# Zero-padded second score products, the mixer's input re-laid through DRAM, and a reorder with one spare tile

## Chip, cores and metric

One core of a Trainium2 chip runs the kernel. TensorE multiplies, VectorE and ScalarE evacuate and do elementwise work, GpSimd helps with small pieces, and nearly all transfers are issued from SyncE's queue (SP). The metric is device time in microseconds (us) of one execution; the median of several runs counts.

## The reference, cut to what matters

Two transformer blocks on a sequence of 1024 tokens of width 1024, in float32. The first has a gated spatial mixer, three groups of dilated window attention and attention to 256 memory tokens. The second has three branches, which the change touches:

```
h = rms_norm(x) * (1 + scale) + shift                     # (1024, 1024)
u, z_ssm, qd, kd, vd, z_diff, qs, ks, vs, z_swa = split(h @ w_in)
# mixer: u is (1024, 16 groups, 16); per group a complex diagonal state of 64
st[t] = a * st[t-1] + B u[t];  y = Re(C st) + d * u;  y = gelu(y) * sigmoid(...)
# differential attention: 4 heads, each two score maps of head dim 64, causal
p = softmax(q1 k1 + bias) - lam * softmax(q2 k2 + bias);  o = rms_norm(p @ v)
# sliding-window attention: 4 query heads on 2 key heads of dim 64, window 128, sinks
x = x + gate * (concat(y_ssm, y_diff, y_swa) @ w_out)
```

## The kernel before

**Precision.** TensorE gets 32-bit values in its fast float32 form, split in two: a high part (hi) and the rest (lo). A dense product is three products, hi x hi, hi x lo and lo x hi, summed in PSUM. ScalarE makes hi by a copy, VectorE lo by a subtraction (`hilo`, and `w_conv` for weights). The normed input lies transposed, channels on partitions, as `hTh` and `hTl` (in the second block `h2Th` and `h2Tl`): 8 tiles of 128 channels x 1024 tokens.

**Units.** `unitA` holds 128 tokens of h as the weights in the array and streams 256 weight columns: 8 x 3 products of 256 columns into PSUM with tokens on partitions. `unitB` holds 128 weight columns and streams 512 tokens: 8 x 3 products of 512 columns, with channels on partitions. A continuation evacuates the PSUM tile.

**The order.** A planner in the kernel (`Sched`) runs coroutines against modelled costs when the program is built, so that the order on each engine is fixed then; the engines execute it in order. Counted resources stand for buffers: `t4` (tiles of 128 x 1024; 20 at first, 24 after `fewer_w` has run twice in the second block), `mm` and `x` (four PSUM tiles each), `raw` (three weight buffers), `whl` (converted weights). `acq` takes them and `rel` gives them back. The dense products are one coroutine, `dense`; a block of attention is one each. The profile gives one line to all instructions of a helper: L239 is a matmul, L249 a transpose, L156 every instruction of VectorE, ScalarE and GpSimd, L253 every transfer. So the tile names tell the place.

**The reorder.** In the first block h is stored with its tokens reordered by a stride of 4 (the second dilation). Group 0 needs plain order. `reorder` does that in place for each of the 8 channel tiles, hi and lo: ScalarE copies hi with a stride into `cvh`, and VectorE copies it back plainly; VectorE copies lo with a stride into `cvl`, and ScalarE copies it back plainly. It holds two spare tiles. TensorE's group 0 products wait for it, and so do the memory products queued beside it.

**The mixer's u.** `dense_u` runs eight `unitA` with the weights being every eighth token of h: unit j takes the tokens 8c + j. ScalarE puts the results into `U` with tokens c on partitions, reversed in j. `ssm` transposes 16 pieces of `U` into `UT`, so that partitions hold 8 steps x 16 channels of a group; from there come input products (`wi`), a scan on VectorE (`scan`, `St`), output products with the tables `T` and `WoZ`, an activation (`Yg`), transposes (`Yn`), and a hi/lo split (`ygh`, `ygl`) that the gated unit (`dense_glu`) reads. The tables are made from powers of a in `ssm_prep`, a stage in the background.

**The second score products.** A query is split into hi and lo, a key too. For differential attention `K[sx]` holds the key's hi in 64 partitions and its lo in the other 64, and `dQh` the query's hi twice, so one product of 128 rows gives hi x hi + hi x lo. The second product, query lo x key hi, takes 64 rows:

```
self.mm(ps[:, :wn], self.dQh[th][:, sx, qs], H.K[sx][:, ks], True, False)
self.mm(ps[:, :wn], self.dQl[hs, th, qs], H.K[sx][hs, ks], False, True)
```

The sliding window does the same with the roles changed: `wQ` holds hi and lo, `wK` hi twice, and `wKl` the key's lo in 64 partitions.

Of the kernel before, what the change touches and what calls it, by code (L numbers as in the profile page):

```python
# [180 lines left out]
class Kern:  # L181
# [508 lines left out]

    def reorder(self, k, ev):

        yield from self.acq("t4", 2)
        for eng, src, name in ((0, self.hTh[:, k], "cvh"), (1, self.hTl[:, k], "cvl")):
            t = self.t4(F32R, name)
            o, i = t.rearrange("p (m r) -> p m r", r=4), src.rearrange("p (r m) -> p m r", r=4).bitcast(F32)
            if eng == 0:
                self.A.activation(o, i, AF.Copy)
                yield
                self.V.tensor_copy(src, t.bitcast(F32))  # L700
            else:
                self.V.tensor_copy(o, i)
                yield
                self.A.activation(src, t.bitcast(F32), AF.Copy)
            yield
        self.rel("t4", 2)
        ev.t = self.s.cur.t

    def bias_prep(self):
# [828 lines left out]
    def ssm_prep(self):  # L1538
# [119 lines left out]

        V.tensor_add(dm, self.ident[0:32, 0:16], self.ident[0:32, 16:32])
        G.memset(Bz, 0.0)  # L1660
        yield
        for pr in range(8):
            tt_ = (tc_, td)[pr % 2]
            EB = tt_[:, 0:256].rearrange("p (c k h) -> p c k h", c=2, k=8)
            CA = tt_[:, 256:544].rearrange("p (c k h) -> p c k h", c=2, k=9)
            we = tt_[:, 544:800]
            Gm = tb[0:32, 768:1024]
            tt = [t2[:, i, 0:128].rearrange("p (a b) -> p a b", a=8) for i in range(2)]
            pb = lambda c, n: pw[:, pr, c, 0:n, None].to_broadcast([P, n, 16])
            self.cmul(EB[:, 0], EB[:, 1], bb[:, 0, pr, None, :].to_broadcast(sh), bb[:, 1, pr, None, :].to_broadcast(sh),  # L1670
                      pb(0, 8), pb(1, 8), tt)
            yield
            yield from self.acq("x")
            ps = self.ps("x")
            for c in range(2):
                self.tr(ps[:, c * P:(c + 1) * P], EB[:, c].rearrange("p a b -> p (a b)"))
            yield
            A.activation(we, ps[:, 0:256], AF.Copy)
            self.rel("x")
            t = self.s.cur.t  # L1680
            self.dma(self.Win_d[:, pr].rearrange("p c q -> p (c q)"), we, 128)
            self.s.cur.t = t
            sh9 = [P, 9, 16]
# [12 lines left out]
            for c in range(2):  # L1696
                self.mm(ps[0:32, 0:P], Bz[:, c, :], CA[:, c, 0:8, :].rearrange("p a b -> p (a b)"), c == 0, c == 1)
            G.memset(Gm[:, 0:P], 0.0)
            yield
            V.tensor_copy(Gm[:, 144:256], ps[0:32, 16:P])  # L1700
            V.scalar_tensor_tensor(Gm[:, P:144], dm, dcol[:, pr:pr + 1], ps[0:32, 0:16], op0=OP.mult, op1=OP.add)
            self.rel("x")
            t = self.s.cur.t
            self.dma(self.G_d[pr], Gm, 32)
            self.s.cur.t = t
            yield
# [165 lines left out]
    def dense_u(self):  # L1872
        s = self.s
        hh, hl = self.hk()
        yield from self.acq("t4", 6)

        U = [self.t4(F32, "U").rearrange("p (g k h) -> p g k h", g=8, k=8) for _ in range(2)]
        left = [8]
        done = Ev()
        w = self.w["u"]  # L1880
        for j in range(8):
            def cont(ps, j=j):
                for i in range(2):
                    self.A.activation(U[i][:, :, 7 - j, :], ps[:, i * P:(i + 1) * P].rearrange("p (g h) -> p g h", g=8),
                                      AF.Copy)
                self.rel("mm")
                left[0] -= 1
                if left[0] == 0:
                    done.t = s.cur.t
                yield  # L1890
            yield from self.unitA(w, hh, hl, slice(j, j + 8 * 127 + 1, 8), self.h_ev if j == 0 else [], cont, 20)
        w.done()
        self.glu_ev = Ev()
        self.zs, self.zs_ev = {}, {}
        s.spawn(self.ssm(U, done), 21, "ssm")

    def ssm(self, U, done):
        I, s, V, A, G = self.I, self.s, self.V, self.A, self.G
        yield done
        yield self.ssmp_ev  # L1900
        A8t = self.cp.tile([P, 7, 3, 8], F32, name="A8")
        self.dma(A8t, self.A8_d, 84)
        gb = self.cp.tile([P, 2], F32, name="glub")
        self.dma(gb, I["glu_b_2"].rearrange("o (e p) -> p (o e)", p=P), 1)
        UT = [self.t4(F32, "UT").rearrange("p (g c) -> p g c", g=8) for _ in range(2)]
        for q in range(4):
            yield from self.acq("x")
            ps = self.ps("x")
            for g in range(4):
                self.tr(ps[:, g * P:(g + 1) * P], U[q // 2][:, q % 2 * 4 + g].rearrange("p k h -> p (k h)"))  # L1910
            yield
            A.activation(UT[q // 2][:, q % 2 * 4:q % 2 * 4 + 4, :], ps.rearrange("p (g c) -> p g c", g=4), AF.Copy)
            self.rel("x")
        self.rel("t4")
        St = [self.t4(F32, "St").rearrange("p (r c) -> p r c", r=8) for _ in range(2)]

# [27 lines left out]
        def load(q):  # L1944
            T, WoZ = Ts[q % 2], Ws[q % 2]
            for k in range(8):

                self.dma(T[16 * k:16 * k + 16],
                         bass.AP(tensor=self.G_d.tensor, offset=self.G_d.offset + q * 2 * 32 * 256 + P - 16 * (7 - k),
                                 ap=[[256, 16], [32 * 256, 2], [16 * 256, 2], [1, P]]), 32)  # L1950
            for s_ in range(2):
                for pr in (2 * q, 2 * q + 1):
                    self.dma(WoZ[pr % 2][s_ * 64:(s_ + 1) * 64, s_], self.Wo_d[s_ * 64:(s_ + 1) * 64, pr], 64)
            yield
            t_ev[q].t = s.cur.t
# [180 lines left out]
    def diff_alloc(self, H):  # L2136
# [5 lines left out]
        H.kalloc.t = self.s.cur.t  # L2142
        if h == 0:

            yield from self.acq("t4", 4)
            self.dbias = self.t4(F32, "dbias")
            self.G.iota(self.dbias, pattern=[[1, 1024]], base=-896, channel_multiplier=-1,
                        allow_small_or_imprecise_dtypes=True)
# [2 lines left out]
            yield  # L2151

            self.dQh = [self.t4(F32R, "dQh").rearrange("p (s t) -> p s t", s=2) for _ in range(2)]
            self.dQl = self.t4(F32R, "dQl").rearrange("p (h t) -> p h t", h=2)
        H.balloc.t = self.s.cur.t
        for th in range(2):
            if h:
# [3 lines left out]
    def dense_diff(self, h, heads):  # L2161
# [42 lines left out]
        def units_q(th):  # L2204
            tsl = slice(th * 512, (th + 1) * 512)

            def cont(ps):
# [3 lines left out]
                for sx in range(2):  # L2211
# [1 line left out]
                    src, q = ps[hs], self.dQh[th][:, sx]  # L2213
                    A.activation(q[hs], src, AF.Copy, scale=f)
                    yield
                    V.scalar_tensor_tensor(self.dQl[hs, th], src, f, q[hs].bitcast(F32), op0=OP.mult, op1=OP.subtract)
                    A.activation(q[64 - sx * 64:128 - sx * 64], src, AF.Copy, scale=f)
                    yield
                self.rel("mm")
# [46 lines left out]
    def diff_block(self, H, i, before):  # L2266
# [21 lines left out]
        def stream(sx):  # L2288
            sc = pr[sx]
            for ch in range(nch):  # L2290
# [2 lines left out]
                wn = max(wd, 256)  # L2293
                yield from self.acq("x")
                ps = self.ps("x")
                qs, ks, hs = slice(i % 4 * P, (i % 4 + 1) * P), slice(c0, c0 + wn), slice(sx * 64, (sx + 1) * 64)
                self.mm(ps[:, :wn], self.dQh[th][:, sx, qs], H.K[sx][:, ks], True, False)
                self.mm(ps[:, :wn], self.dQl[hs, th, qs], H.K[sx][hs, ks], False, True)
                yield
                bo = 896 - i * P + c0  # L2300
                V.tensor_tensor_reduce(out=sc[:, c0:c0 + wd], in0=ps[:, :wd], in1=self.dbias[:, bo:bo + wd], scale=1.0,
# [70 lines left out]
        if H.left == 0:  # L2372
# [1 line left out]
            self.spill_y(2 + h, H.z)  # L2374
            self.rel("t4", 3)
            if h == 3:
                self.rel("t4", 4)

    def z_alloc(self, H):
        yield from self.acq("t4")  # L2380
# [10 lines left out]

    def swa_alloc(self, W_):
        I, V, G = self.I, self.V, self.G
        yield from self.acq("t4", 3)

        W_.K, W_.Kl = [self.t4(F32R, "wK") for _ in range(2)], self.t4(F32R, "wKl")
        W_.kalloc.t = self.s.cur.t
        yield from self.acq("t4", 1)
        W_.V = self.t4(F32, "wV").rearrange("p (b v) -> p b v", b=8)
# [18 lines left out]
    def dense_swa(self, H3):  # L2418
# [8 lines left out]
        for th in range(2):  # L2427
            tsl = slice(th * 512, (th + 1) * 512)

            def cont(ps, th=th, tsl=tsl):  # L2430
                yield W_.kalloc
                for sx in range(2):
# [2 lines left out]
                    hi = W_.K[sx][hs, tsl]  # L2435
                    A.activation(hi, src, AF.Copy)
                    yield
                    V.tensor_sub(W_.Kl[hs, tsl], src, hi.bitcast(F32))
                    A.activation(W_.K[sx][64 - sx * 64:128 - sx * 64, tsl], src, AF.Copy)
                    yield  # L2440
                self.rel("mm")
# [68 lines left out]
    def swa_block(self, W_, b, before):  # L2510
# [19 lines left out]
        def pair(kv):  # L2530
            yield from self.acq("x")
            psS = self.ps("x").rearrange("p (s k) -> p s k", s=2)
            for sx in range(2):
                q, hs = W_.Q[th][kv][:, sx, b % 4 * P:(b % 4 + 1) * P], slice(kv * 64, (kv + 1) * 64)
                self.mm(psS[:, sx, :], q, W_.K[kv][:, c0:c0 + 256], True, False)
                self.mm(psS[:, sx, :], q[hs], W_.Kl[hs, c0:c0 + 256], False, True)
            yield
            for sx in range(2):
                h = 2 * kv + sx
# [37 lines left out]
        if W_.left[th] == 0:  # L2577
            self.rel("t4", 2)
            if th:
                self.rel("t4", 7)  # L2580
        yield
        while (th, 1) not in self.wz_ev:
            yield lambda: (th, 1) in self.wz_ev
# [229 lines left out]
```

## Time and profile before

| | |
|---|---|
| median of 3 runs | 1868.13 us (1867.87 to 1875.78) |
| profiled execution | 1873.96 us, span 1871.5 us |
| TensorE busy | 1826.0 us (98%) |
| VectorE, ScalarE, GpSimd busy | 54%, 38%, 7% |
| TensorE's mean granted clock | 0.977 of 2.4 GHz |
| moved by DMA | 145.80 MB |

Busy time counts from the start to the end of instructions; those of TensorE overlap, so its pace is read from start to start. The span is the time from the first to the last instruction; the execution's own time is a little longer.

### The profile page before, as it was taken

The page shows a single profiled execution, that of the slowest core. Times are in us where ns is not written, and L with a number is a line of the kernel's source. Part 1 is how long each engine was busy: PE and PEld are TensorE (multiplying, and loading weights), DVE is VectorE, ACT ScalarE, POOL GpSimd, SP SyncE. Part 2 cuts the span into 40 slices and gives each one's busy share as a digit, 9 for nine tenths or more (in the row PEclk, how much of TensorE's full clock was granted, in tenths as well). Part 3 has the DMA queues.
Part 4 walks back from the last instruction along what each step waited for, and adds up shares of the span by engine and source line. Part 5 has one row for each costly group of instructions (what it writes and reads, how often), then busy time and mean ns, then how long its engine had stood idle before and what let it go on. Part 6 is the DMA issues. An engine that isn't in the chain of part 4 may idle for free.

```text
span 1871.5 us, 28564 instructions
## 1 busy us (share of the span) xinstructions
PE 1826.0 (98%) x11071; PEld 1599.5 (85%) x11071; DVE 1007.1 (54%) x2674; ACT 713.3 (38%) x1648; POOL 136.2 (7%) x203
## 2 busy tenths in 40 slices
PE   7999599999999999999999999999999999999998
PEld 6999599998899878878888889999877687777798
DVE  5657755655666776521322334550486735554575
ACT  5454753543414222111211222661334434534543
POOL 1313202210000000000000000010000000000000
PEclk9999799999999999999999999999999998998899
DMA  6212131112232225611212212530202110101442
GB/s 217 73 64 69 35 114 46 35 37 68 71 117 61 57 65 165 197 48 46 91 45 77 76 62 91 170 117 14 68 29 57 46 57 12 46 23 68 168 139 76
DMA packets 163722, 145.80 MB, mean 78 GB/s; under 512 B 17996, under 2 KB 149630, under 8 KB 163588
## 3 DMA queue, kind: packets, MB, share of 16 engines
q1 hardware_dynamic: 163588, 143.99, 24.6%
q8 instruction: 87, 1.43, 0.3%
q14 instruction: 47, 0.39, 0.1%
HBM read 123.57 MB, written 22.75 MB: 78 GB/s over the span
## 4 chain that ended last, share of the span: by engine, by line
PE 94%; DVE 3%; ACT 2%; DMA 1%; issue 0%; SPq 0%; POOLq 0%; POOL 0%; DVEq 0%; ACTq 0%
PE psmm L239 76%; PE psx L239 13%; PE psx L249 4%; ACT cvh L156 1%; DMA xt<-in_x_dram 1%; DVE dp L156 1%; DMA t<-in_rel_bias_dram 0%; ACT wsc L156 0%; SPq L253 0%; ACT hTl L156 0%; DVE Q L156 0%; ACT dp L156 0%; DVE zs L156 0%; DVE wlo L156 0%; DVE dst L156 0%
## 5 line engine op out<-in xcount | busy, mean ns | idle before, releaser
L156 DVE TENSOR_TENSOR wlo<-wraw,whi 128x1024 fp32r<-128x1024 f32 (+3 forms) x161 | 183.2, 1138 | 224.5 <-ACT whi L156 215.7
L239 PE MATMUL psmm<-hTh,whi 128*128 128x512 f32 x672 | 266.0, 396 | 0.0
L239 PE MATMUL psmm<-whi,hTh 128*128 128x256 f32 x896 | 263.4, 294 | 1.4 <-ACT hTh L156 1.4
L239 PE MATMUL psmm<-hTl,whi 128*128 128x512 f32 x672 | 262.0, 390 | 0.0
L239 PE MATMUL psmm<-hTh,wlo 128*128 128x512 f32 x672 | 262.0, 390 | 0.0
L239 PE MATMUL psmm<-whi,hTl 128*128 128x256 f32 x896 | 254.9, 284 | 0.0
L239 PE MATMUL psmm<-wlo,hTh 128*128 128x256 f32 x896 | 254.7, 284 | 0.0
L239 PEld LDWEIGHTS psmm<-whi,hTh 128*128 128x128 f32 x896 | 173.8, 194 | 2.5 <-ACT hTh L156 1.8
L239 PEld LDWEIGHTS psmm<-wlo,hTh 128*128 128x128 f32 x896 | 174.1, 194 | 0.1
L239 PEld LDWEIGHTS psmm<-whi,hTl 128*128 128x128 f32 x896 | 173.6, 194 | 0.2 <-DVE hTl L156 0.2
L156 ACT ACTIVATE whi<-wraw 128x1024 fp32r<-128x1024 f32 (+3 forms) x161 | 158.7, 989 | 33.8 <-PE psmm L239 19.3
L239 PEld LDWEIGHTS psmm<-hTh,wlo 128*128 128x128 f32 x672 | 126.2, 188 | 26.9
L239 PEld LDWEIGHTS psmm<-hTh,whi 128*128 128x128 f32 x672 | 126.2, 188 | 26.6 <-issue 1.8
L239 PEld LDWEIGHTS psmm<-hTl,whi 128*128 128x128 f32 x672 | 126.3, 188 | 24.6
L156 ACT ACTIVATE tg<-psmm,gb 128x512 f32<-128x512 f32 x48 | 33.1, 689 | 283.2 <-PE psmm L239 258.6
L239 PE MATMUL psmm<-h2Th,whi 128*128 128x512 f32 x320 | 140.3, 439 | 0.0
L239 PE MATMUL psmm<-h2Tl,whi 128*128 128x512 f32 x320 | 129.5, 405 | 0.0
L239 PE MATMUL psmm<-h2Th,wlo 128*128 128x512 f32 x320 | 129.3, 404 | 0.0
L156 POOL TENSOR_TENSOR hst<-hst,mhalf 128x4 f32<-128x4 f32 (+1 forms) x68 | 68.5, 1011 | 257.8 <-DVE hst L156 246.1
L239 PEld LDWEIGHTS psmm<-h2Th,whi 128*128 128x128 f32 x320 | 62.7, 196 | 18.5 <-issue 7.3
L239 PEld LDWEIGHTS psmm<-h2Th,wlo 128*128 128x128 f32 x320 | 62.7, 196 | 14.4
L156 DVE CUSTOM_DVE_ANT_0 dp<-psx,dbias 128x512 f32<-128x512 f32 (+3 forms) x96 | 52.6, 555 | 40.7 <-PE psx L239 39.7
(355 smaller groups left out, 3817.7 us busy)
## 6 DMA issues: line engine op xcount, KB each, us to landing
wraw<-in_w_in_dram SPq DMA_DIRECT2D x96, 512.0 KB
wraw<-in_w_out_dram SPq DMA_DIRECT2D x32, 512.0 KB
ada<-in_ada_w_dram SPq DMA_DIRECT2D x24, 512.0 KB
wraw<-in_m_w_kv_dram SPq DMA_DIRECT2D x8, 512.0 KB
x2t<-in_x_dram SPq DMA_DIRECT2D x8, 512.0 KB
x_d<-x2t SPq DMA_DIRECT2D x8, 512.0 KB
xt<-in_x_dram SPq DMA_DIRECT2D x7, 512.0 KB
og_d<-rows SPq DMA_DIRECT2D x24, 132.0 KB
```

Of the source, the lines that this page charges most:

```text
L156: r = real(*a, **k)
L239: self.nc.tensor.matmul(out, lhsT, rhs, start=start, stop=stop)
L249: self.nc.tensor.transpose(out, in_, self.ident[:k, :k])
```

## The change

1. `reorder`: for hi and lo in turn, ScalarE copies the tile plainly into one spare tile, and VectorE copies it back with the stride.
2. `dense_u`: four `unitB` instead of eight strided `unitA`. ScalarE writes the PSUM tile with tokens regrouped (j, c) into `U`; each half of `U` is stored to DRAM (`u0_d`, `u1_d`), and `ssm` loads it back in 8 pieces of 16 partitions as `UT`. The 16 transposes go. Since the order of the 8 steps isn't reversed any more, the tables are made from reversed powers (`pwr`) and loaded in the other order.
3. The second score products take 128 rows: `dQl` and `wKl` become a pair of tiles each, in which the 64 partitions not used are set to zero once. One more `t4` is held for each pair.

```
 def reorder(self, k, ev):
+        for src in (self.hTh[:, k], self.hTl[:, k]):
+            yield from self.acq("t4")
+            t = self.t4(F32R, "cv")
+            self.A.activation(t, src.bitcast(F32), AF.Copy)
+            yield
+            self.V.tensor_copy(src.rearrange("p (m r) -> p m r", r=4),
+                               t.rearrange("p (r m) -> p m r", r=4).bitcast(F32))
+            yield
+            self.rel("t4")
...
+        pwr = tc_[:, 800:928].rearrange("p (r c k) -> p r c k", r=8, c=2)
+        for k in range(8):
+            V.tensor_copy(pwr[:, :, :, k], pw[:, :, :, 7 - k])
...
 def dense_u(self):
+        for e in range(2):
+            left = [2]
+            for th in range(2):
+                def cont(ps, e=e, th=th, left=left):
+                    self.A.activation(U[e][:, :, th * 64:(th + 1) * 64], ps.rearrange("p (c j) -> p j c", j=8), AF.Copy)
+                    self.rel("mm")
+                    left[0] -= 1
+                    if left[0] == 0:
+                        yield
+                        self.dma(self.u_d[e], U[e].rearrange("p j c -> p (j c)"))
+                        done[e].t = s.cur.t
+                    yield
+                yield from self.unitB(w, slice(e * P, (e + 1) * P), hh, hl, slice(th * 512, (th + 1) * 512),
+                                      [self.h_ev[4 * th + 3]] * 8, cont, 20)
...
 def ssm(self, done):
+        for e in range(2):
+            yield done[e]
+            for j in range(8):
+                self.dma(UT[e][16 * j:16 * j + 16], bass.AP(tensor=self.u_d[e].tensor, offset=self.u_d[e].offset + j * P,
+                                                            ap=[[S, 16], [16 * S, 8], [1, P]]), 64)
-        for q in range(4):
-            yield from self.acq("x")
-            ps = self.ps("x")
-            for g in range(4):
-                self.tr(ps[:, g * P:(g + 1) * P], U[q // 2][:, q % 2 * 4 + g].rearrange("p k h -> p (k h)"))
...
 def diff_alloc(self, H):
-            yield from self.acq("t4", 4)
+            yield from self.acq("t4", 5)
+            self.dQl = [self.t4(F32R, "dQl").rearrange("p (h t) -> p h t", h=2) for _ in range(2)]
+            for sx in range(2):
+                self.G.memset(self.dQl[sx][64 - sx * 64:128 - sx * 64].bitcast(F32), 0.0)
...
 def diff_block(self, H, i, before):
-                self.mm(ps[:, :wn], self.dQl[hs, th, qs], H.K[sx][hs, ks], False, True)
+                self.mm(ps[:, :wn], self.dQl[sx][:, th, qs], H.K[sx][:, ks], False, True)
...
 def swa_alloc(self, W_):
-        yield from self.acq("t4", 3)
+        yield from self.acq("t4", 4)
+        W_.K, W_.Kl = [[self.t4(F32R, n) for _ in range(2)] for n in ("wK", "wKl")]
+        for sx in range(2):
+            G.memset(W_.Kl[sx][64 - sx * 64:128 - sx * 64].bitcast(F32), 0.0)
...
 def swa_block(self, W_, b, before):
-                self.mm(psS[:, sx, :], q[hs], W_.Kl[hs, c0:c0 + 256], False, True)
+                self.mm(psS[:, sx, :], q, W_.Kl[kv][:, c0:c0 + 256], False, True)
```

## Rows read from the trace of the kernel before

**Rows 1.** The page: busy us, share of the span and instructions of each engine.

```profile
PE 1826.0 (98%) x11071; PEld 1599.5 (85%) x11071; DVE 1007.1 (54%) x2674; ACT 713.3 (38%) x1648; POOL 136.2 (7%) x203
```

**Rows 2.** Busy time by stretch: length, engines, granted clock, DMA share, GB/s.

```profile
200.00:240.00 40.00, 20.12 (x97) 16.21 (x96) 31.34 (x97) 34.08 (x68) 5.84 (x10) 0.62 0.12 37
...
1340.00:1400.00 60.00, 60.00 (x271) 44.97 (x270) 53.96 (x186) 19.89 (x47) 2.97 (x5) 1.00 0.09 27
...
1500.00:1700.00 200.00, 198.93 (x991) 154.28 (x990) 98.37 (x299) 84.05 (x200) 11.80 (x21) 0.96 0.11 35
1700.00:1776.00 76.00, 75.92 (x380) 59.21 (x381) 36.35 (x134) 36.17 (x107) 0.00 (x0) 0.82 0.35 122
```

**Rows 3.** Timeline of TensorE at 1342 us: start, duration, instruction.

```profile
1342.43 0.49 PE L239 MATMUL psx<-dK,dQl 64*128 64x512 f32 x1
1342.86 0.49 PE L239 MATMUL psx<-dK,dQh 128*128 128x512 f32 x1
...
1343.70 0.50 PE L239 MATMUL psmm<-h2Th,whi 128*128 128x512 f32 x1
1344.04 0.39 PE L239 MATMUL psmm<-h2Tl,whi 128*128 128x512 f32 x1
1344.27 0.39 PE L239 MATMUL psmm<-h2Th,wlo 128*128 128x512 f32 x1
```

**Rows 4.** The same at 1696 us, sliding-window scores, fourteen rows of the pattern left out.

```profile
1696.28 0.28 PE L239 MATMUL psx<-wK,wQ 128*128 128x256 f32 x1
1696.49 0.38 PE L239 MATMUL psx<-wKl,wQ 64*128 64x256 f32 x1
...
1701.17 0.58 PE L239 MATMUL psx<-wK,wQ 128*128 128x256 f32 x1
1701.68 0.58 PE L239 MATMUL psx<-wKl,wQ 64*128 64x256 f32 x1
```

**Rows 5.** The same at 196 us, scores of the first block.

```profile
196.84 0.64 PE L239 MATMUL psx<-K,Q 128*128 128x256 f32 x4
197.31 0.28 PE L239 MATMUL psmm<-whi,hTh 128*128 128x256 f32 x1
```

**Rows 6.** By tile, dQl and wKl: ns min/median/max, first and last start, forms.

```profile
L239 PE MATMUL psx<-dK,dQl x96: 379/492/793, 1335.6 to 1675.3; 64*128 64x512 f32 x48, 64*128 64x256 f32 x32, 64*128 64x384 f32 x16
...
L239 PE MATMUL psx<-wKl,wQ x32: 378/481/581, 1696.5 to 1752.7; 64*128 64x256 f32 x32
```

**Rows 7.** By tile, U.

```profile
L156 ACT ACTIVATE U<-psmm x16: 272/275/277, 1276.9 to 1317.5; 128x128 f32<-128x128 f32 x16
...
L249 PE MATMUL psx<-ident,U x16: 272/273/273, 1319.3 to 1320.9; 128*128 128x128 f32 x16
```

**Rows 8.** Timeline of TensorE at 1317 us, where the products of u end.

```profile
1316.91 0.41 PE L239 MATMUL psmm<-whi,h2Tl 128*128 128x256 f32 x1
1317.16 0.28 PE L239 MATMUL psmm<-whi,h2Th 128*128 128x256 f32 x1
1317.28 0.28 PE L239 MATMUL psmm<-wlo,h2Th 128*128 128x256 f32 x1
```

**Rows 9.** Busy time by stretch, while the mixer's tables are loaded.

```profile
1328.00:1344.00 16.00, 16.00 (x104) 12.18 (x103) 6.48 (x24) 4.99 (x23) 0.00 (x0) 1.00 0.34 90
```

**Rows 10.** By tile, ygl and ygh: the mixer's end and the gated unit.

```profile
L156 DVE TENSOR_TENSOR ygl<-psx,ygh x4: 672/685/691, 1447.0 to 1454.7; 128x512 fp32r<-128x512 f32 x4
...
L239 PE MATMUL psmm<-ygh,whi x8: 389/436/502, 1460.0 to 1469.1; 128*128 128x512 f32 x8
```

**Rows 11.** By tile, cvh and cvl: the reorder's copies.

```profile
L156 ACT ACTIVATE cvh<-hTh x8: 1948/1998/2097, 197.6 to 222.7; 128x1024 fp32r<-128x1024 f32 x8
L156 DVE CAST hTh<-cvh x8: 683/694/695, 205.9 to 230.3; 128x1024 fp32r<-128x1024 f32 x8
...
L156 DVE CAST cvl<-hTl x8: 1164/1204/1312, 209.0 to 235.4; 128x1024 fp32r<-128x1024 f32 x8
L156 ACT ACTIVATE hTl<-cvl x8: 1047/1058/1071, 211.4 to 236.6; 128x1024 fp32r<-128x1024 f32 x8
```

**Rows 12.** Timeline of TensorE at 228 us, with the idle time before and what ended it.

```profile
228.18 1.22 PE L239 MATMUL psx<-K,Q 128*128 128x256 f32 x4 [10.67 <-DVE Q L156]
```

More of the change, by code (lines that the diff above doesn't have):

```diff
@@ L691, in reorder @@
     def reorder(self, k, ev):
[L693 to L704, printed above, removed]
+        for src in (self.hTh[:, k], self.hTl[:, k]):
+            yield from self.acq("t4")
+            t = self.t4(F32R, "cv")
+            self.A.activation(t, src.bitcast(F32), AF.Copy)
             yield
-        self.rel("t4", 2)
+            self.V.tensor_copy(src.rearrange("p (m r) -> p m r", r=4),
+                               t.rearrange("p (r m) -> p m r", r=4).bitcast(F32))
+            yield
+            self.rel("t4")
         ev.t = self.s.cur.t
@@ L1670, in ssm_prep @@
             self.cmul(EB[:, 0], EB[:, 1], bb[:, 0, pr, None, :].to_broadcast(sh), bb[:, 1, pr, None, :].to_broadcast(sh),
-                      pb(0, 8), pb(1, 8), tt)
+                      *(pwr[:, pr, c, :, None].to_broadcast(sh) for c in range(2)), tt)
             yield
@@ L1875, in dense_u @@
         yield from self.acq("t4", 6)
-        U = [self.t4(F32, "U").rearrange("p (g k h) -> p g k h", g=8, k=8) for _ in range(2)]
-        left = [8]
-        done = Ev()
+        U = [self.t4(F32, "U").rearrange("p (j c) -> p j c", j=8) for _ in range(2)]
+        self.u_d = [self.dp.tile([P, S], F32, name=f"u{e}_d") for e in range(2)]
+        done = [Ev(), Ev()]
         w = self.w["u"]
[L1881 to L1891, printed above, removed]
+        for e in range(2):
[12 more added lines that the diff above has]
+                                      [self.h_ev[4 * th + 3]] * 8, cont, 20)
         w.done()
@@ L1894, in dense_u, with ssm @@
         self.zs, self.zs_ev = {}, {}
-        s.spawn(self.ssm(U, done), 21, "ssm")
-    def ssm(self, U, done):
+        s.spawn(self.ssm(done), 21, "ssm")
+    def ssm(self, done):
         I, s, V, A, G = self.I, self.s, self.V, self.A, self.G
-        yield done
+        UT = [self.t4(F32, "UT").rearrange("p (g c) -> p g c", g=8) for _ in range(2)]
+        for e in range(2):
[4 more added lines that the diff above has]
+            yield
         yield self.ssmp_ev
@@ L1904, in ssm @@
         self.dma(gb, I["glu_b_2"].rearrange("o (e p) -> p (o e)", p=P), 1)
-        UT = [self.t4(F32, "UT").rearrange("p (g c) -> p g c", g=8) for _ in range(2)]
-        for q in range(4):
-            yield from self.acq("x")
-            ps = self.ps("x")
-            for g in range(4):
-                self.tr(ps[:, g * P:(g + 1) * P], U[q // 2][:, q % 2 * 4 + g].rearrange("p k h -> p (k h)"))
-            yield
-            A.activation(UT[q // 2][:, q % 2 * 4:q % 2 * 4 + 4, :], ps.rearrange("p (g c) -> p g c", g=4), AF.Copy)
-            self.rel("x")
         self.rel("t4")
@@ L1948, in load @@
                 self.dma(T[16 * k:16 * k + 16],
-                         bass.AP(tensor=self.G_d.tensor, offset=self.G_d.offset + q * 2 * 32 * 256 + P - 16 * (7 - k),
+                         bass.AP(tensor=self.G_d.tensor, offset=self.G_d.offset + q * 2 * 32 * 256 + P - 16 * k,
                                  ap=[[256, 16], [32 * 256, 2], [16 * 256, 2], [1, P]]), 32)
@@ L2153, in diff_alloc @@
             self.dQh = [self.t4(F32R, "dQh").rearrange("p (s t) -> p s t", s=2) for _ in range(2)]
-            self.dQl = self.t4(F32R, "dQl").rearrange("p (h t) -> p h t", h=2)
+            self.dQl = [self.t4(F32R, "dQl").rearrange("p (h t) -> p h t", h=2) for _ in range(2)]
+            for sx in range(2):
+                self.G.memset(self.dQl[sx][64 - sx * 64:128 - sx * 64].bitcast(F32), 0.0)
         H.balloc.t = self.s.cur.t
@@ L2215, in cont @@
                     yield
-                    V.scalar_tensor_tensor(self.dQl[hs, th], src, f, q[hs].bitcast(F32), op0=OP.mult, op1=OP.subtract)
+                    V.scalar_tensor_tensor(self.dQl[sx][hs, th], src, f, q[hs].bitcast(F32), op0=OP.mult, op1=OP.subtract)
                     A.activation(q[64 - sx * 64:128 - sx * 64], src, AF.Copy, scale=f)
@@ L2295, in stream @@
                 ps = self.ps("x")
[L2296 removed]
+                qs, ks = slice(i % 4 * P, (i % 4 + 1) * P), slice(c0, c0 + wn)
                 self.mm(ps[:, :wn], self.dQh[th][:, sx, qs], H.K[sx][:, ks], True, False)
[L2298 removed]
+                self.mm(ps[:, :wn], self.dQl[sx][:, th, qs], H.K[sx][:, ks], False, True)
                 yield
@@ L2376, in diff_block @@
             if h == 3:
-                self.rel("t4", 4)
+                self.rel("t4", 5)
     def z_alloc(self, H):
@@ L2393, in swa_alloc @@
         I, V, G = self.I, self.V, self.G
-        yield from self.acq("t4", 3)
-        W_.K, W_.Kl = [self.t4(F32R, "wK") for _ in range(2)], self.t4(F32R, "wKl")
+        yield from self.acq("t4", 4)
+        W_.K, W_.Kl = [[self.t4(F32R, n) for _ in range(2)] for n in ("wK", "wKl")]
+        for sx in range(2):
+            G.memset(W_.Kl[sx][64 - sx * 64:128 - sx * 64].bitcast(F32), 0.0)
         W_.kalloc.t = self.s.cur.t
@@ L2437, in cont @@
                     yield
-                    V.tensor_sub(W_.Kl[hs, tsl], src, hi.bitcast(F32))
+                    V.tensor_sub(W_.Kl[sx][hs, tsl], src, hi.bitcast(F32))
                     A.activation(W_.K[sx][64 - sx * 64:128 - sx * 64, tsl], src, AF.Copy)
@@ L2533, in pair @@
             for sx in range(2):
-                q, hs = W_.Q[th][kv][:, sx, b % 4 * P:(b % 4 + 1) * P], slice(kv * 64, (kv + 1) * 64)
+                q = W_.Q[th][kv][:, sx, b % 4 * P:(b % 4 + 1) * P]
                 self.mm(psS[:, sx, :], q, W_.K[kv][:, c0:c0 + 256], True, False)
-                self.mm(psS[:, sx, :], q[hs], W_.Kl[hs, c0:c0 + 256], False, True)
+                self.mm(psS[:, sx, :], q, W_.Kl[kv][:, c0:c0 + 256], False, True)
             yield
@@ L2579, in swa_block @@
             if th:
-                self.rel("t4", 7)
+                self.rel("t4", 8)
         yield
```

## The prediction

> **What bounds the kernel now.** I read the page's engine shares first: TensorE is busy for 98% of the span [rows 1], so a change counts as far as it shortens TensorE's own queue or one of its few gaps. A busy engine may still be slow, so next came the busy times by stretch with the granted clock [rows 2]: between 200 and 240 us TensorE does nothing for half the time, and after 1500 us the clock is not always full. Third came TensorE's timeline in the three places that the change touches, read from start to start, because the ends of matmuls overlap. The reader is to see three spacings. A 512-wide score product beside one of 64 rows starts 0.43 us after the last, while plain 512-wide products follow each other at 0.23 us [rows 3]. Sixteen 256-wide score products of alternating 128 and 64 rows take 4.89 us from the first start to the start after the last, 0.306 us each, and at the lower clock 0.51 us [rows 4]. The attention of the first block makes the same hi and lo products with all 128 rows; four start within 0.47 us, 0.12 us each [rows 5]. So it is the alternation of row counts that costs, not the width or the change of weights.
>
> **Score products on 128 rows.** There are 96 second products in the differential attention, 48 of 512, 32 of 256 and 16 of 384 columns, and 32 of 256 in the sliding-window attention [rows 6]. Each is one of a pair with a 128-row product, and the pair pays twice. A 256-wide pair falls from 2 x 0.306 to 2 x 0.12, by 0.37 us; a 512-wide pair from 2 x 0.43 to 2 x 0.23, by 0.40 us [rows 3 to 5]. For 384 columns no plain row exists; it lies between the two, so I take 0.38. Sum: 64 x 0.37 + 48 x 0.40 + 16 x 0.38 = 23.7 + 19.2 + 6.1 = **49 us**. The plain product after a pair also starts 0.34 instead of 0.23 us later [rows 3]; I leave this out as reserve.
>
> A rule speaks against this. The Trainium skill, "TensorE: Matmul & The Clock Gate", Part 3 (packing small matmuls), says that products on different row groups can run at the same time, so that a half-height product can be nearly free; padding would give that up. By it this term would be a loss, worked out below as a rival. The rows here show 0.31 and 0.43 us for every half-height product and no overlap [rows 3, 4], because a full-height one stands on either side of it.
>
> **The clock.** It is 0.96 in the 200 us after 1500 and 0.82 in the 76 us after 1700 [rows 2]; 8.0 and 13.7 us of full-speed time are not granted, 21.7 in all. In the timeline the fall to 1.2 GHz at 1701 comes at the end of the sixteen alternating products [rows 4]; the plain work before that ran at 2.4 GHz. If the alternation goes, most of these falls should go. Bounds: nothing and 21.7 us. I take two thirds, **14 us**, since some falls may follow real waits.
>
> **What the other engines keep.** The work around the scores hangs on VectorE, which is busy 54 of 60 us between 1340 and 1400 [rows 2]. The 49 us lie over 418 us (1335 to 1753, [rows 6]), so 7 us fall into that stretch, and VectorE leaves 6. In the sliding-window part VectorE and ScalarE are half idle, but each block is a chain through both. Bounds: nothing lost, and 20 us, the 7 there and as much in either later stretch; I take **7 us lost**. The zeroed halves are memsets on GpSimd, which is busy for 7% of the span [rows 1], and stand once each.
>
> **The products of u.** Now eight units read every eighth token as weights; their evacuations run from 1276.9 to 1317.5 us [rows 7], two to a unit, so a unit is about 40.6 / 7 = 5.80 us, 0.242 us for each of 24 products, at full clock. The moment the weights are contiguous again, the same 256-wide product starts every 0.12 us [rows 8]; the stride, not the clock, halves the rate. The new form has the weights still and contiguous and streams 512 tokens: 4 units x 24 x 0.23 = 22.1 us [rows 3] against 8 x 5.80 = 46.4: **24.3 us** less. The 16 transposes go too; they run from 1319.3 to 1320.9 us [rows 7]: **1.7 us**. All of it stands on TensorE with nothing else running.
>
> **u through memory.** The mixer now waits for a 512 KB store and eight 64 KB loads for each half. The nearest rows are the mixer's own small loads: 90 GB/s in the 16 us after 1328 [rows 9]. The second half, 0.5 MB out and 0.5 MB back, is at that rate 5.8 + 5.8 = 12 us, against some 4 us now from the last u evacuation to the transposed copy; so the mixer is about 8 us later as seen from TensorE's queue. SP's queue waits meanwhile (the loads wait for the store), and the weight loads behind it are late by as much; three raw buffers, each of 11 us of products (2 x 24 x 0.23), cover that. What is late next is the gated unit that reads the mixer: its last input is written at 1454.7 + 0.7 and TensorE reaches it at 1460.0, 4.6 us to spare [rows 10]. TensorE will come to it earlier: 49 x 125 / 418 = 15 us of the pair saving lie before 1460. If VectorE's scan didn't get any faster, TensorE would stand there for 8 + 15 - 4.6 = 18 us; but VectorE also waits for scores in that stretch, and the planner knows of the transfers and can put other work in front. Bounds 0 and 18 us; I take **4 us lost**. The reversed powers are eight small VectorE copies in a background stage, covered by dense products.
>
> **The reorder.** ScalarE now makes 8 strided copies of 2.00 and 8 plain ones of 1.06 us, VectorE 8 of 1.20 and 8 of 0.69 [rows 11]. After it ScalarE makes 16 plain ones (17.0 instead of 24.5 us) and VectorE 16 strided ones (19.2 instead of 15.1). They stand where TensorE idles for 20 of 40 us, ScalarE is busy for 34.1 and VectorE for 31.3 [rows 2]; the longest gap, 10.7 us, ends with a Q piece that stood behind reorder copies on ScalarE [rows 12]. ScalarE falls to 26.6, VectorE rises to 35.4. The stretch shortens at most to what VectorE needs, 4.6 us; at worst VectorE's 4.1 us are added. Nearest to the rows is relief of the fuller engine: **4 us** less. Holding one spare tile instead of two can only free tiles earlier.
>
> **Tiles.** Two longer-held tiles (the second dQl, the second wKl) leave less room in a pool of 24 while head 1 is set up. The wait would stand in the dense queue before head 1's gate product. I count 25 tiles wanted there; head 0's blocks end close to it and return four. Taken as nothing; bound 11 us, the length of that gate product's two units.
>
> **Sum.** The profiled execution took 1873.96 us with a span of 1871.5. 49 + 14 - 7 + 26 - 4 + 4 = 82 us less gives 1792. The median of the runs shown is 5.8 us below the profiled one, so the forecast against it is 1868.1 - 82 = **1786 us**.
>
> **Rivals.**
> (1) The mixer and VectorE become the bound: TensorE is faster but stands before the gated unit and in the scan stretch. For it: 4.6 us to spare [rows 10], VectorE at 90%. Against: VectorE waits for scores there. Losses of 18 + 20 instead of 4 + 7 us, and no clock gained: 1786 + 27 + 14 = 1827 at its worst, about 1812 in the middle.
> (2) Padding doesn't do what it says: the stall stays, for instance because it comes from the change of weights. Then only u and the reorder help: 1868 - 26 = 1842. Against: [rows 5].
> (3) Half-height products were nearly free and each now costs its full time: 64 x 0.12 + 48 x 0.23 + 16 x 0.18 = 21.6 us more; with u and the reorder 1868 + 22 - 26 = 1864, no change. [rows 3, 4] speak against it, since nothing overlaps there. It is the packing rule of the Trainium skill, "TensorE: Matmul & The Clock Gate", Part 3, named above.
> (4) Slower: the re-laid u lands so late that TensorE, whose queue is in order, stands at the mixer's input products. The place is the first product that reads UT; every microsecond late there costs one. It decides from 82 us on. To be that late the sixteen 64 KB loads would have to land one after the other at over 5 us each. The mixer's small loads moved 1.4 MB in 16 us [rows 9], which speaks against it.
>
> **How the numbers follow.** Forecast 0.70 (its own range 1766 to 1804: all of the clock and no loss, or no clock gain and small losses); rival 1 0.17; rival 2 0.06; rival 3 0.03; rival 4 0.04. The range from 1764 to 1822 holds the forecast and most of rival 1. A measurement of this kernel tells about 0.5%, 9 us, from no change: faster 0.93, same 0.03, slower 0.04.
>
> **What the profile after would show.** Second products of 128 rows at 0.12 and 0.23 us from start to start; a clock near 1.00 after 1500; u as four units of 5.5 us; ScalarE's reorder copies all near 1.06 us and VectorE's near 1.20; little idle time on TensorE before the ygh products. A long idle row there, or in front of the products that read UT, would make the forecast wrong, as would scores that keep a spacing of 0.3 us.

## The result and the profile after

The changed kernel took 1785.37 us (median of 4 runs, 1783.57 to 1786.1) against 1868.0 for before: a ratio of 0.9549, with a 95% interval from 0.9521 to 0.9578. The profiled execution took 1786.1 us with a span of 1784.3, against 1871.5.

The page's engine shares and then the windows of after (length, engines, granted clock, DMA share, GB/s), which answer to [rows 1, 2]:

```profile
PE 1733.3 (97%) x10959; PEld 1552.2 (87%) x10959; DVE 1008.6 (57%) x2682; ACT 701.5 (39%) x1632; POOL 143.7 (8%) x207
```

```profile
200.00:240.00 40.00, 21.49 (x131) 18.67 (x130) 34.53 (x89) 27.05 (x72) 12.27 (x11) 0.66 0.12 37
1340.00:1400.00 60.00, 59.03 (x348) 50.74 (x347) 50.26 (x170) 27.84 (x63) 2.20 (x4) 1.00 0.20 58
1500.00:1700.00 200.00, 193.65 (x1159) 168.94 (x1158) 130.25 (x409) 110.86 (x279) 12.65 (x21) 0.98 0.24 80
1680.00:1700.00 20.00, 16.94 (x118) 16.35 (x119) 13.96 (x27) 9.62 (x21) 0.00 (x0) 0.83 0.34 110
```

TensorE has 112 instructions fewer, 96 products of u and the 16 transposes; the rest is the same work in less time: 93 us less busy, and 5.5 us more idle. The 0.98 after 1500 us is no longer a fall among the score products; it comes from the last 20 us, behind a wait, to which we come back.

TensorE's timeline of after, in the differential attention and in the sliding window, against [rows 3, 4]:

```profile
1301.34 0.28 PE L239 MATMUL psx<-dK,dQh 128*128 128x256 f32 x1
1301.46 0.28 PE L239 MATMUL psx<-dK,dQl 128*128 128x256 f32 x1
...
1508.36 0.39 PE L239 MATMUL psx<-dK,dQh 128*128 128x512 f32 x1
1508.59 0.39 PE L239 MATMUL psx<-dK,dQl 128*128 128x512 f32 x1
1508.82 0.40 PE L239 MATMUL psx<-dK,dQh 128*128 128x512 f32 x1
...
1659.27 0.28 PE L239 MATMUL psx<-wKl,wQ 128*128 128x256 f32 x1
1659.39 0.28 PE L239 MATMUL psx<-wK,wQ 128*128 128x256 f32 x1
```

From start to start it is 0.12 us for 256 columns and 0.23 for 512; 0.31 and 0.43 are gone.

By tile (ns min/median/max, first and last start), the copies of u, the mixer's end, the gated unit and the reorder, against [rows 7, 10, 11]:

```profile
L156 ACT ACTIVATE U<-psmm x4: 598/598/599, 1272.5 to 1288.9; 128x512 f32<-128x512 f32 x4
...
L156 DVE TENSOR_TENSOR ygl<-psx,ygh x4: 679/683/691, 1411.5 to 1421.6; 128x512 fp32r<-128x512 f32 x4
...
L239 PE MATMUL psmm<-ygh,whi x8: 389/389/475, 1430.7 to 1437.0; 128*128 128x512 f32 x8
...
L156 ACT ACTIVATE cv<-hTh x8: 1042/1046/1059, 196.9 to 215.0; 128x1024 fp32r<-128x1024 f32 x8
L156 DVE CAST hTh<-cv x8: 1180/1220/1253, 202.8 to 223.9; 128x1024 fp32r<-128x1024 f32 x8
```

A unit of u is now (1288.9 - 1272.5) / 3 = 5.47 us. The gated unit has not become a wait: its last input is written at 1421.6 + 0.7 and read at 1430.7, 8.4 us to spare instead of 4.6.

The new idle time stands where the forecast did not look. TensorE at the end of the sliding window, after (start, duration, instruction, idle time before it and what ended it):

```profile
1674.27 0.41 PE L249 MATMUL psx<-ident,wsc 128*128 128x128 f32 x2 [0.94 <-DVE wst L156]
...
1679.36 0.41 PE L249 MATMUL psx<-ident,wsc 128*128 128x128 f32 x2 [0.94 <-DVE wsc L156]
1682.20 0.58 PE L239 MATMUL psmm<-whi,yh 128*128 128x256 f32 x1 [2.43 <-ACT yh L156]
1682.58 0.42 PE L239 MATMUL psmm<-wlo,yh 128*128 128x256 f32 x1
1683.67 0.80 PE L239 MATMUL psmm<-whi,yh 128*128 128x256 f32 x2 [0.67 <-DVE yh L156]
```

Products of 256 columns that last 0.28 us elsewhere last 0.58 behind that wait: TensorE was granted the lower level, 1.2 GHz, for some 7 us (0.83 on the average of the 20 us from 1680).

### The profile page after: what moved, and what is told of

The parts are those of the page before. It is cut to its first block, busy times and chain, and to the rows that moved or that the text cites. A ratio compares the mean times of both kernels' runs of the same rounds, so it can differ in the third digit from the quotient of the medians.

```text
span 1784.3 us, 28346 instructions
## 1 busy us (share of the span) xinstructions
PE 1733.3 (97%) x10959; PEld 1552.2 (87%) x10959; DVE 1008.6 (57%) x2682; ACT 701.5 (39%) x1632; POOL 143.7 (8%) x207
## 4 chain that ended last, share of the span: by engine, by line
PE 90%; DVE 5%; ACT 2%; DMA 1%; issue 1%; POOL 0%; SPq 0%; POOLq 0%; DVEq 0%; ACTq 0%
PE psmm L239 76%; PE psx L239 10%; PE psx L249 4%; DVE dp L156 1%; ACT cv L156 1%; DVE hTl L156 1%; DVE scan L156 1%; DMA ada<-in_ada_w_dram 1%; DVE wlo L156 0%; DMA xt<-in_x_dram 0%; ACT whi L156 0%; DVE macc L156 0%; DVE zs L156 0%; DVE dK L156 0%; ACT dp L156 0%
## 5 line engine op out<-in xcount | busy, mean ns | idle before, releaser
L239 PE MATMUL psmm<-h2Th,wlo 128*128 128x512 f32 x352 | 138.0, 392 | 0.0
L239 PE MATMUL psmm<-h2Tl,whi 128*128 128x512 f32 x352 | 137.8, 391 | 0.0
L156 POOL TENSOR_TENSOR hst<-hst,mhalf 128x4 f32<-128x4 f32 (+1 forms) x68 | 69.4, 1024 | 259.4 <-DVE hst L156 247.9
L239 PEld LDWEIGHTS psmm<-h2Th,whi 128*128 128x128 f32 x352 | 66.5, 189 | 11.8 <-issue 0.2
L239 PEld LDWEIGHTS psmm<-h2Tl,whi 128*128 128x128 f32 x352 | 66.6, 189 | 10.6
```

Source lines behind the costliest of these rows:

```text
L156: r = real(*a, **k)
L239: self.nc.tensor.matmul(out, lhsT, rhs, start=start, stop=stop)
```

## The experiments

In the first four, the parts alone and a test of the stall's cause, before took 1872.68 us on the same chip.

**Padding alone.** Part 3 of the change:

```
-self.mm(ps[:, :wn], self.dQl[hs, th, qs], H.K[sx][hs, ks], False, True)
+self.mm(ps[:, :wn], self.dQl[sx][:, th, qs], H.K[sx][:, ks], False, True)
```

> Before, with the second score products padded to 128 rows and nothing else. Theory A, changing the row count stalls TensorE and the falls of the clock follow from these stalls: from the traces of before and after, 37.5 us of pair spacing and 3 us of late plain products at full clock, plus 24 us of half-clock time, less about 7 us of new idle time at the end: 1868 - 58 = 1810 us (1800 to 1818), granted clock near 1.00 after 1500 us. Theory B, the falls of the clock have another cause: only 41 us less, 1827 to 1834 us, and the clock stays near 0.82 in the last stretch before the output products. Theory C, the stall belongs to the change of weights: 1868 us.

1819.26 us (1818.15 to 1820.0), ratio 0.972 (0.9687 to 0.9754). Its windows:

```profile
1500.00:1700.00 200.00, 198.79 (x1150) 172.12 (x1150) 121.02 (x397) 105.64 (x268) 12.63 (x21) 1.00 0.17 53
1700.00:1764.00 64.00, 58.82 (x472) 57.46 (x471) 40.64 (x91) 29.44 (x73) 1.10 (x2) 0.95 0.48 165
```

The clock is 1.00 through the scores, so theory A, though 1 us beyond its range; against before on this chip it is 53 us less, where A had 58. TensorE stands idle for 15.9 us in the second block instead of 5.2, while A allowed for 7. Part of that stands at the mixer's transposes (four waits of 0.5 to 1.4 us), part is the 2.43 us wait on yh, the same as in after. In the two parts below that wait does not appear, so it comes with the padding.

**u alone.** Part 2 of the change:

```
-yield from self.unitA(w, hh, hl, slice(j, j + 8 * 127 + 1, 8), self.h_ev if j == 0 else [], cont, 20)
+yield from self.unitB(w, slice(e * P, (e + 1) * P), hh, hl, slice(th * 512, (th + 1) * 512), ..., cont, 20)
```

> Before, with u as four units and the way through memory alone; score products stay on 64 rows. Theory A, the transfers are covered: 46.4 - 22.1 + 1.7 = 26 us less, 1842 us (1838 to 1846). Theory B, the mixer arrives 8 us later against 4.6 us to spare at the gated unit, and TensorE stands there: 1846 to 1852 us, with an idle row of 3 us or more in front of the ygh products.

1847.96 us (1842.58 to 1852.38), ratio 0.9873 (0.9834 to 0.9912): 24 us less, with 17 to 31 in the interval. The time lies in B's range, but both ranges were set from 1868 us, and 1872.68 - 26 = 1847 is what A gives on this chip. The trace decides, with the mixer's end at 1436.8 + 0.7 and the gated unit at 1447.9, 10.4 us to spare and no idle row before it. Theory A.

```profile
L156 DVE TENSOR_TENSOR ygl<-psx,ygh x4: 679/683/686, 1426.6 to 1436.8; 128x512 fp32r<-128x512 f32 x4
...
L239 PE MATMUL psmm<-ygh,whi x8: 387/486/500, 1447.9 to 1455.6; 128*128 128x512 f32 x8
```

**The reorder alone.** Part 1 of the change:

```
-self.A.activation(o, i, AF.Copy)
-self.V.tensor_copy(src, t.bitcast(F32))
...
+self.A.activation(t, src.bitcast(F32), AF.Copy)
+self.V.tensor_copy(src.rearrange("p (m r) -> p m r", r=4), t.rearrange("p (r m) -> p m r", r=4).bitcast(F32))
```

> Before, with the reorder alone. Theory A, ScalarE's relief is worth what the landmarks of before and after show between 154 and 588 us: 4 us less, 1864 us (1862 to 1866). Theory B, it is an accident of the planner's order with the other two edits, or only the 0.8 us earlier start: 1867 to 1870 us.

1865.82 us, ratio 0.9983 (0.9962 to 1.0004): 3 us less, not clear of noise by the time. By the trace the last product of whi and hTh starts 575.5 us after the first transpose (584.8 - 9.3) instead of 579.0 (588.6 - 9.6), 3.5 us earlier. The other traces agree: 575.1 to 575.5 us in four with these copies (after and two edits of it among them), 578.0 to 579.2 us in four without. So A, by the traces.

**Fewer changes of row count.** Before, with every other pair reversed:

```
-self.mm(psS[:, sx, :], q, W_.K[kv][:, c0:c0 + 256], True, False)
-self.mm(psS[:, sx, :], q[hs], W_.Kl[hs, c0:c0 + 256], False, True)
+hi, lo = (q, W_.K[kv][:, c0:c0 + 256]), (q[hs], W_.Kl[hs, c0:c0 + 256])
+first, last = (hi, lo) if sx else (lo, hi)
+self.mm(psS[:, sx, :], *first, True, False)
+self.mm(psS[:, sx, :], *last, False, True)
```

(and the other way round in the differential attention).

> Before, with 64-row second products kept, but every other pair reversed (first, second, second, first), so that where pairs adjoin, equal row counts adjoin and the changes of row count are halved. Theory A, each change of row count costs: a 64-row product behind a 64-row one starts at most 0.12 us (256 columns) or 0.23 us (512) after it, and the time falls by up to half of 42 us and of 24 us of clock: 1833 to 1855 us. Theory B, each 64-row product costs by itself: spacing and time stay, 1868 us. Theory C, products on different halves of the rows overlap: the second 64-row product starts 0.05 us or less after the first.

1832.79 us (1832.12 to 1834.53), ratio 0.9794 (0.9761 to 0.9828), with the same 128 products of 64 rows. Its timeline (x2 is two instructions in one row):

```profile
1671.49 0.50 PE L239 MATMUL psx<-wK,wQ 128*128 128x256 f32 x2
1671.91 0.39 PE L239 MATMUL psx<-wKl,wQ 64*128 64x256 f32 x2
1672.23 0.50 PE L239 MATMUL psx<-wK,wQ 128*128 128x256 f32 x2
...
1677.55 0.38 PE L239 MATMUL psx<-wKl,wQ 64*128 64x256 f32 x1
1677.86 0.50 PE L239 MATMUL psmm<-h2Th,whi 128*128 128x512 f32 x1
```

Two things are to be seen. A cycle of four products takes 1672.23 - 1671.49 = 0.74 us instead of 4 x 0.306 = 1.22, with two changes of row count instead of four; so each change costs some 0.2 us, and theory A holds. And two 64-row products take 0.32 us to the next start where one takes 0.31: the second is nearly free, as in theory C; one by one in the trace, it starts 0.003 us after the first. The two stand on different halves of the rows and write different PSUM tiles. B, by which spacing and time stay, falls.

The changes were not halved in all: where other work came between the pairs they did not adjoin. In the trace 39 of the 128 products of 64 rows stand right behind another, and the changes fell from 256 to 178. That the time still came out just below A's range is the clock, of which all came back and not half. One reading is left open. The same times follow if a 64-row product costs by itself and two on different halves share that cost, since each group of them has a change at either end; no run puts two on the same half side by side. For counting it makes no difference here.

Its clock, where [rows 2] has 0.96 and 0.82:

```profile
1500.00:1700.00 200.00, 199.37 (x1066) 157.56 (x1065) 107.23 (x341) 94.90 (x235) 10.73 (x19) 1.00 0.14 45
1700.00:1777.00 77.00, 76.92 (x574) 70.64 (x573) 54.56 (x147) 41.17 (x107) 1.10 (x2) 1.00 0.48 165
```

**The changed kernel and three edits of it**, on one chip, where before took 1866.82 us.

> The changed kernel as it stands, as the measure for the next three on the same chip: 1785 us (1783 to 1787) by every theory, with executions within 3 us of each other, since the falls of the clock are gone.

1785.38 us (1784.29 to 1785.75).

**Gate and gain later.**

```
 if th == 0:
+    while (2, 0) not in yh:
+        yield lambda: (2, 0) in yh
     s.spawn(rows(), 25, "rows")
```

> The changed kernel, but the two gate and gain tiles of the output are taken only after the third pair of stored results has its three tiles. Theory A, the wait for yh at 1682 us (2.4 + 0.7 us, and the half clock behind it) is want of tiles, because the padded wKl holds one more: 3 to 6 us less, 1779 to 1782 us, and no idle row on yh. Theory B, the end of the sliding window sets this place in any case: 1784 to 1787 us, and the wait stands at another tile.

1777.78 us (1777.16 to 1781.04), 7.6 us less than after; the ratio to before is 0.9526 (0.9501 to 0.955). SP's queue of after, and then of this kernel:

```profile
1628.32 1.88 SPq L253 DMA_DIRECT2D yr<-y_d  x4
1630.30 0.38 SPq L253 DMA_DIRECT2D gate<-mod_d  x1
...
1671.82 5.70 SPq L253 DMA_DIRECT2D yr<-y_d  x8
```

```profile
1626.81 5.14 SPq L253 DMA_DIRECT2D yr<-y_d  x6
...
1673.44 0.51 SPq L253 DMA_DIRECT2D gate<-mod_d  x1
```

Before, the same loads stood in this order:

```profile
1699.95 2.88 SPq L253 DMA_DIRECT2D yr<-y_d  x6
...
1769.27 0.36 SPq L253 DMA_DIRECT2D gate<-mod_d  x1
```

In after the gate takes the free tiles at 1630, and the third pair of results, which needs three, waits for 41 us. Before loaded all six at 1699.9 and the gate at 1769. With the order restored there is no idle row on yh, and between 1680 and 1700 the clock is 1.00 instead of 0.83:

```profile
1680.00:1700.00 20.00, 20.00 (x169) 20.00 (x169) 16.16 (x35) 9.09 (x23) 0.00 (x0) 1.00 0.51 184
```

Theory A; I had priced the wait and little of the low clock behind it, and the gain came out above the range.

**Lo copies on GpSimd.**

```
+if src is lo:
+    self.G.tensor_copy(t, src.bitcast(F32))
+else:
     self.A.activation(t, src.bitcast(F32), AF.Copy)
```

> The changed kernel, with the plain copies of the lo tiles in the reorder on GpSimd instead of ScalarE. Theory A, TensorE's 6.2 us wait at 215 us is for score pieces behind the reorder copies on ScalarE: 8.4 us less on ScalarE there, 2 to 5 us less in all, 1780 to 1783 us. Theory B, VectorE's 19 us of strided copies set the stretch: 1784 to 1787 us.

1793.1 us (1789.63 to 1794.37), 7.7 us slower than after: neither theory. By tile and in TensorE's timeline:

```profile
L156 POOL CAST cv<-hTl x8: 1030/1502/1854, 211.2 to 229.7; 128x1024 fp32r<-128x1024 f32 x8
L156 DVE CAST hTl<-cv x8: 1123/1229/1876, 213.0 to 233.9; 128x1024 fp32r<-128x1024 f32 x8
```

```profile
217.87 1.11 PE L239 MATMUL psx<-bV,sc 128*128 128x64 f32 x4 [9.40 <-ACT sc L156]
...
228.51 1.11 PE L239 MATMUL psx<-bV,sc 128*128 128x64 f32 x4 [9.09 <-DVE rows L156]
```

GpSimd starts 3.1 us later than ScalarE did and takes 1.50 us a copy; the last piece comes back 4.1 us later, with two waits of over 9 us. The planner made another order for it too, so the engine alone is not what was measured.

**The store of u made twice.**

```
+self.nc.sync.dma_start(u2_d[e], U[e].rearrange("p j c -> p (j c)"))
+self.nc.sync.dma_start(U[e].rearrange("p j c -> p (j c)"), u2_d[e])
 self.dma(self.u_d[e], U[e].rearrange("p j c -> p (j c)"))
```

> The changed kernel with the store of each half of u made twice, with a load back between the two stores, which the planner does not know of; the order of all instructions stays. The first product that reads UT comes some 6 us later. Theory A, the way through memory is covered, with 8.4 us to spare at the gated unit: 1785 to 1788 us. Theory B, the mixer is on the path, and each microsecond late costs one: 1790 us or more.

1790.48 us (1789.69 to 1790.8), 5.1 us more than after. The last load of u is issued at 1305.4 instead of 1297.6, 7.8 us later. TensorE's timeline at the input products, first of after, then of this kernel:

```profile
1306.96 2.02 PE L239 MATMUL psx<-UT,wi 128*64 128x128 f32 x32
...
1314.74 0.66 PE L239 MATMUL psx<-UT,wi 128*64 128x128 f32 x8
```

```profile
1309.32 0.67 PE L239 MATMUL psx<-UT,wi 128*64 128x128 f32 x8 [2.17 <-DVE dp L156]
1310.36 2.85 PE L239 MATMUL psx<-UT,wi 128*64 128x128 f32 x24 [0.37 <-DMA wi<-Win_d]
...
1318.67 0.67 PE L239 MATMUL psx<-UT,wi 128*64 128x128 f32 x8
```

The cost falls at the input products, and the last group of these starts 3.9 us late (1318.7 for 1314.7): of 7.8 us, 3.9 were covered. At the gated unit there are still over 8 us to spare. So B in size, but at another place than the gated unit: the loads of wi stand behind those of u in SP's queue, at 1306.7 instead of 1298.9.

**The walk of the reorder's copies**, where before took 1872.68 us. First ScalarE permutes by writing every fourth element:

```
-self.A.activation(t, src.bitcast(F32), AF.Copy)
+self.A.activation(t.rearrange("p (m r) -> p r m", r=4), src.rearrange("p (r m) -> p r m", r=4).bitcast(F32), AF.Copy)
-self.V.tensor_copy(src.rearrange("p (m r) -> p m r", r=4), t.rearrange("p (r m) -> p m r", r=4).bitcast(F32))
+self.V.tensor_copy(src, t.bitcast(F32))
```

> The changed kernel, but in the reorder ScalarE makes the permutation, reading plainly and writing every fourth element, and VectorE copies back plainly; the order of the instructions stays. Theory A, ScalarE pays for a stride on the side that it reads and not on the side that it writes: its copies stay near 1.06 us, VectorE's fall from 1.20 to 0.69 us, 8 us less on the engine that is busy for 28 of 30 us between 200 and 230: 2 to 6 us less, 1779 to 1783 us. Theory B, a stride costs on either side: ScalarE's copies take 2.0 us, 15 us more on it, 1790 us or more.

1796.34 us (1794.82 to 1797.31), so theory B. With it and the later gate and gain:

> The same reorder and the later gate and gain tiles together. If the two are independent: 1777.8 us less what the first gives by theory A, 1772 to 1776 us, or by theory B 1782 us or more.

1789.82 us (1787.05 to 1796.14); 1796.3 - 7.6 = 1788.7 is what independence gives with B. And VectorE walking the other way (`"p (m r) -> p r m"` on the side written, `"p (r m) -> p r m"` on the side read):

> The changed kernel, with VectorE's copies of the reorder walked in the other order: plain reads and writes of every fourth element, instead of reads 256 elements apart and plain writes. Theory A, VectorE pays for the distance on the side that it reads: 0.69 us each and 2 to 6 us less, 1779 to 1783 us. Theory B, any stride takes it out of its fast form: 1.2 us each, 1784 to 1787 us.

1785.14 us (1783.58 to 1787.47), no difference from after, as theory B has it. The copies by tile and two of TensorE's waits with ScalarE's permutation, then the copies with VectorE's other walk:

```profile
L156 ACT ACTIVATE cv<-hTh x8: 2006/2062/2105, 197.6 to 228.1; 128x1024 fp32r<-128x1024 f32 x8
...
215.29 0.69 PE L249 MATMUL psx<-ident,sc 128*128 128x128 f32 x2 [8.98 <-ACT sc L156]
228.30 1.12 PE L239 MATMUL psx<-bV,sc 128*128 128x64 f32 x4 [12.32 <-ACT sc L156]
```

```profile
L156 DVE CAST hTh<-cv x8: 1075/1100/1127, 202.9 to 223.4; 128x1024 fp32r<-128x1024 f32 x8
```

ScalarE pays 2.06 us for writing every fourth element as it paid 2.00 for reading 256 elements apart [rows 11]; VectorE pays 1.10 for the one and 1.20 for the other. The plain copies take 1.06 and 0.69 us, so neither side is spared.

**Contiguous weights for u.**

```
-hh, hl, slice(j, j + 8 * 127 + 1, 8), ...
+hh, hl, slice(j * P, (j + 1) * P), ...
```

> Before, with each of the eight units of u reading 128 neighbouring tokens as weights instead of every eighth; u then holds its tokens in another order, so the mixer computes another sequence. Theory A, the stride of the weights halves the rate: 0.12 us for each product of 256 columns, 2.9 us a unit, 23 us less, 1845 us, and then the way through memory gains only by making the order right. Theory B, the shape (tokens as weights, 256 columns) is slow: 5.8 us a unit, 1868 us.

1846.54 us (two runs, 1839.41 and 1853.68); the timing is rough, the trace is not:

```profile
L156 ACT ACTIVATE U<-psmm x16: 272/275/278, 1273.9 to 1294.2; 128x128 f32<-128x128 f32 x16
```

(1294.2 - 1273.9) / 7 = 2.90 us a unit against 5.80: the stride alone halves the rate, theory A.

## Why the forecast held, point by point

The forecast of 82 us was made against the profiled execution. There the span fell by 87.2; the medians differ by 82.6, since the profiled execution of before had a lower clock than most. On its own ground the forecast was 5 us short; that 1786 met 1785.4 is luck, because it was set against the median of before, which had less low clock to lose. I took both timelines of TensorE and summed, from the first h2 product to the first Y product, what each product took from start to start above the plain spacing (0.12, 0.18 and 0.232 us by width).

| term | forecast | measured |
|---|---|---|
| pairs at full clock, and the plain product behind them | -49 | 39.4 to 2.0, and 3.0 to 0: **-40.4** |
| products at half clock | -14 | 24.9 to 2.8, and 1.5 in 256-wide dense products: **-23.6** |
| products and transposes of u | -26 | 8 x 5.80 - 4 x 5.47 + 1.7: **-26.2** |
| reorder | -4 | first transpose to last whi, hTh, 579.0 to 575.1: **-3.9** |
| idle (VectorE 7, mixer 4) | +11 | 5.2 to 12.0: **+6.8** |

The sum is -87.3, against 87.2 us by the span.

**Pairs.** The mechanism holds. The first two rows do not part the time as the forecast did: its sum took every pair at full clock, and 34 score products of before (by their spacing; 40 by the granted clock at their start) ran at half clock and stand, stall and all, in the second row. Counted as the forecast counted the clock, by time not granted after 1500 us, that fell from 21.7 us [rows 2] to 200 x 0.02 = 4, by 18 us. That leaves 46 us to the pairs instead of 49, of which 3 are the plain products behind them, left out as reserve. At full clock a pair of before cost 0.35 us on the average at either width, where the sum had 0.37 and 0.40.

**Clock.** Too small by 4 us in that count: all falls among the scores went, not two thirds. Both experiments that took changes of row count away, by padding and by order alone, have 1.00 between 1500 and 1700 us; u alone and the reorder alone, which keep all 256 changes, have 0.95 and 0.96 there. So the alternation brought on these falls, and with 178 changes none of them was left. The longest that remains in after, 7 us, begins in the wait on yh and went with it. Rival 2, a stall from the change of weights, falls with them: the weights change as often in all these kernels.

**u.** Right in size, and the stride is shown to be the cause.

**Reorder.** Right in size by the traces. That relief of ScalarE is what counts there is borne out by the walk: with ScalarE's copies back at 2.06 us and VectorE's plain, the kernel took 11 us more, and TensorE waited 9.0 and 12.3 us for score pieces from ScalarE.

**u through memory.** The step that failed is where the mixer would be waited for. It is not the gated unit, whose margin grew to 8.4 us: the mixer from its first input product to its last ygl takes (1422.3 - 1307.0) = 115 us instead of (1455.4 - 1325.5) = 130. VectorE no longer waits so long for scores, and padding alone makes it 119 us; but u alone, with the scores as before, makes it 123, so that is not the whole, and the rest stays open. The place is the products that read UT, which rival 4 named, and 3.9 us were covered there. So the 4 us were not lost, and rival 1 is wrong here.

**VectorE.** Not lost in 1340 to 1400 either (59.0 of 60 us busy on TensorE); 5 us of idle time stand at the end of the sliding window. So the 11 us of these two terms met 6.8 us that arose elsewhere, and it is luck that the sizes are near.

**Tiles.** "Taken as nothing" was the other step that failed. The padding brings a shortage, not at head 1 but at the output products, and with the low clock behind it it costs 7.6 us, inside the bound of 11. That the tile is wKl's is read from the code, where dQl's has been given back by then; the run with padding alone has both.

**Rival 3** failed on these rows, and the experiment on order says why its rule is nevertheless sound. The Trainium skill, "TensorE: Matmul & The Clock Gate", Part 3 (packing small matmuls), lets products on different row groups overlap. The trace agrees where two 64-row products adjoin: 0.32 us for both. The Trainium skill, "TensorEngine Tiling (Array Packing)", Tiling Modes, says that changing the tiling mode, not only the tile, drains the engine. The stall agrees, some 0.2 us at each change by the experiment on order. Before had a change on either side of every half-height product.

## What to carry to other kernels

A matmul with fewer rows between full ones is not cheap: count the changes of row count, about 0.2 us each here, and either pad with zeros or put the small ones side by side (here 1819 us the one and 1833 the other). Read strided weights as a rate, not a layout detail: they halved a stage of 46 us. After an edit that holds one more buffer, look for who takes the last free one: a small load that was early by 40 us cost 7.6 us, and the version with it held back, 1777.78 us, beats both kernels.

## What the runs showed that I had not expected

- The falls of the clock make the times scatter. Nine executions of before on one chip ran from 1862.53 us at a mean granted clock of 0.984 to 1875.87 at 0.976; five of after on the same chip lie within 1.5 us at 0.987 to 0.988. The padded and the reordered pairs alone have the same calm (1.9 and 2.4 us), u and the reorder alone do not (9.8 and 8.6 us).
- Two 64-row products on different halves of the rows start 0.003 us apart and take 0.32 us to the next start; one takes 0.31.
- GpSimd's plain copy of 128 x 1024 took 1.50 us, ScalarE's 1.05.
